# A hybrid decoder step on one core: the keys of heads 6 and 7 computed as a pair of column blocks, their queries projected later, four logit pages moved

## The chip, the cores and the metric

The kernel runs on one core of one Trainium2 chip; the other cores are idle. The metric is device time in microseconds (us): the median over runs of the whole program, lower is better. A core has five engines that run their own instruction streams in order and wait for one another by semaphores: TensorE (PE, matrix products, with PEld for its weight loads), VectorE (DVE), ScalarE (ACT), GpSimd (POOL) and SyncE (SP, which only issues transfers). Accumulators of TensorE are banks of a memory called PSUM.

## The reference

One layer of a decoder step on 528 prompt rows (512 and 16 learned meta rows) and 32 sample rows (8 sequences of 4). Everything is float32.

```
h = rmsnorm(x, g_pre)
q, k, v, ga, cb, cc, ch, gc, ma, mc = split(h @ w_in)     # 2048 x 12288
a = stick_breaking(q, k, v) * silu(ga)                     # 8 heads of 128, strictly causal
c = cb * causal_conv(cc * ch) * silu(gc)
merged = sigmoid(ma + b) * (a @ w_pa) + sigmoid(mc + b) * (c @ w_pc)
y = x + rmsnorm(merged @ w_out, g_post)
```

`stick_breaking` takes logits `z = q.k / sqrt(128) + b_h` and weighs value `s` for query `t` by `sigmoid(z_ts)` times the product of `1 - sigmoid(z_tj)` over the keys `j` between them, in log space. The prompt attends to itself. Each sample sequence attends to 512 cached keys and values (four pages of 128, found by a page table) and to its own four rows. The new keys and values are outputs too.

## The kernel before

**Products.** A float32 matrix is split into two parts of a faster format, `hi` and `lo`, and a product is made of three matrix products: `hi*hi`, `hi*lo`, `lo*hi`. A block of weights is 128 rows of 8 tiles (a `raw` tile, 512 KB). `w_split` (lines 250 to 255) makes `whi` on ScalarE (line 253) and `wlo` on VectorE (line 254); three buffers of each exist (`whl`, line 85: `bufs=3`), so the fourth block has to wait until TensorE has used the first.

**Solo and pair.** A column block of 128 columns of `w_in` costs 2 blocks of weights by 8 tiles by 3 products by 2 halves of the rows: 96 matrix instructions (`gemm`, line 269 of the profile). Two neighbouring column blocks can be done together by `seven` (line 1096, through `pair`, line 1137): a scheme of Strassen's kind, with 7 block products instead of 8, each of 24 instructions (line 1091 of the profile), 168 for two column blocks. It needs sums of weights, made by VectorE into `s` and `raw` (lines 1111 to 1129), sums of the activations (`t_hi`, `t_lo`, made once by `t_sums` and `t_parts`), and differences of results (`c`, lines 1127 and 1132). A pair uses two accumulators `mm` and one `o`; there are three `mm` banks in turn and one `o` bank:

```
def mm_ps():
    return ps.tile([P, 512], F32, tag="mm", name="mm", bufs=3)
```

**Stages.** In order: norm and the queries of heads 0 to 3; `head_now` for heads 0 to 3 (keys, values, the queries of head 4 + h, then the attention of head h); solo column blocks for the keys and values of heads 4 and 5 and the keys of heads 6 and 7 (`tiles`, line 1050), between which the activation sums are made (`STEPS`, line 1056); the values of heads 6 and 7 as the first pair (`later_pair`, line 797); 4 pairs for `ga`, 16 for the convolution, 16 for the gates `ma` and `mc`; then the attention of heads 4 to 7 among the products with `w_pc`, the products with `w_pa`, and `w_out`.

**The samples' attention** (`decode_steps`, line 827) is spread over these stages by `dec_step`. Its first part takes 64 steps, here called pages: one page of cached keys for four heads, 16 instructions on VectorE (line 849, `junk` and `z_all` from `kpage` and `qb`), each a dot product of 128 by 128. `DEC1` and `PAGES` (lines 48 and 779) put the first 5 units of 4 pages behind heads 0 to 3; `dec_group` (line 977), called after each pair, issues the others. When all pages are done, VectorE adds the bias to all logits (lines 879 and 882), ScalarE runs the softplus functions on them (lines 519 to 522) under a function table of its own, and TensorE makes the running sums (lines 895 to 902). Since ScalarE would otherwise change tables again and again, `behind_gates` (line 958) puts the softplus behind the latest sigmoids of the gates, and line 1247 puts each later sigmoid behind the softplus; a sigmoid is also what reads an `mm` or `o` bank of a `ma`/`mc` pair and frees it.

The order of the instructions on each engine is made when the program is built: a scheduler takes what is ready by its own estimates, in the order of the program text where two are ready. On the chip each engine keeps that order.

Of the kernel before, what the change touches and what calls it, by code (L numbers as in the profile page):

```python
# [17 lines left out]
P = 128  # L18
# [24 lines left out]
H = 8  # L43
# [1 line left out]
NPG = 4  # L45
NPOOL = 40
EPS = 1e-6
DEC1 = 5
SCRATCH = 4096
FIRST = 4  # L50
WARM = 8
# [10 lines left out]
def hybrid_step_kernel(  # L62
# [584 lines left out]
    def k_store(h, kr):  # L647
        pool.dma_start(k_scr[h], kr)
# [127 lines left out]
                              start=False, stop=(g == GROUPS[-1] and i == 2), skip_group_check=True)  # L776
        yield ot

    PAGES = ((1, 1, 2, 2), (1, 1, 2, 1), (1, 1, 2, 1), (1, 1, 1, 1))

    def head_now(h):

        qr = hp.tile([P, TQ], F32, name="qr", bufs=2)[:, 0:PQ]
        nc.sync.dma_start(qr, qt_scr[h][:, 0:PQ])
        khi, klo = k_split(np_, k_proj(h))
        dec_step(PAGES[h][0], "part")
        vhi, vlo = v_split(np_, v_proj(h))
        dec_step(PAGES[h][1], "part")
        q_proj(NOW + h)
        dec_step(PAGES[h][2], "part")  # L790
        ot = next(attend(np_, h, khi, klo, vhi, vlo, *q_split(np_, qr)))
        dec_step(PAGES[h][3], "part")
        at = hp.tile([P, TQ], F32, name="qr", bufs=2)[:, 0:PQ]
        act.copy(at, ot)
        pool.dma_start(a_scr[h], at)

    def later_pair(c, h, ready):

        raws = [hp2.tile([P, T], F32, name="raw", bufs=2) for _ in range(2)]
        seen = []  # L800
        for m, half, b in pair(c + h * P, HC, ready):
            act.copy(raws[m][:, NMETA + half * HQ:NMETA + (half + 1) * HQ], b[:, HM:])
            act.copy(raws[m][:, half * HM:(half + 1) * HM], b[:, :HM])
            seen.append(m)
            if seen.count(m) == 2:
                v_store(h + m, v_out(hp2, h + m, raws[m]))

    def head_loads(h, pl):
# [168 lines left out]
    def dec_group():  # L977

        n = n_group[0] = n_group[0] + 1
        if n <= 27:  # L980
            dec_step((0, 2, 2, 2)[n - 1] if n <= 4 else 1 if n <= 20 else 4, "logits")
        else:
            dec_step(2 if n <= 30 else 1)

# [33 lines left out]
    with tc.tile_pool(name="tsum", bufs=2, side="right") as tsp:  # L1018
        r1 = tsp.tile([P, 8, HC], F32, name="r1", bufs=1)

        first_sum = sp2.tile([P, 8, P], F32, name="s")
        held = {}

        def part(x, c, *ij):
            return (blk(x, *ij) if ij else x)[:, c:c + 2]

        def whole(out, c, *ij):
            pin(dve.tensor_add(out, part(h_f, c, *ij), part(l_f, c, *ij)))

        def t_sums(c):  # L1030

            x, y = held[c] = [tsp.tile([P, 2, HC], F32, name=n) for n in "xy"]
            r = part(r1, c)
            whole(y, c, 0, 0)
            whole(r, c, 0, 1)
            pin(dve.tensor_sub(r, y, r))
            whole(x, c, 1, 1)
            pin(dve.tensor_add(x, r, x))
            pin(dve.tensor_sub(y, y, x))

        def t_parts(c):

            x, y = held.pop(c)
            z = tsp.tile([P, 2, HC], F32, name="z", bufs=1)
            whole(z, c, 1, 0)
            pin(dve.tensor_sub(z, z, x))
            for i, src in enumerate((x, y, z)):
                t_split(part(t_hi[i], c), part(t_lo[i], c), src)

        tiles = [(c, h) for h in range(NOW, SOLO) for c in (GATE_K, GATE_V)] + [(GATE_K, h) for h in range(SOLO, H)]  # L1050

        def unit(i, u, pin=lambda ins: ins):
            return w_split(w_load(win_srcs(tiles[i][0] + tiles[i][1] * P)[u]), pin)

        units = {(0, u): unit(0, u) for u in range(2)}
        STEPS = ((), (), ((t_sums, 0), (t_sums, 2)), ((t_parts, 0), (t_sums, 4), (t_parts, 2)),
                 ((t_sums, 6), (t_parts, 4)), ((t_parts, 6),))
        for i, (c, h) in enumerate(tiles):
            if i:
                units[i, 1] = unit(i, 1, pin)  # L1060
            o = gemm([units[i, u] for u in range(2)], h_rhs, ALL)
            if i + 1 < len(tiles):
                units[i + 1, 0] = unit(i + 1, 0, pin)
            for step, n in STEPS[i]:
                step(n)
            if i + 1 == len(tiles):
                first_ws = blocks_of(win, GATE_V + SOLO * P)
                pin(dve.tensor_add(first_sum, first_ws[1], first_ws[2]))
                for n in range(0, 8, 2):
                    t_split(blk(h_hi, 0, 1)[:, n:n + 2], blk(h_lo, 0, 1)[:, n:n + 2], r1[:, n:n + 2])  # L1070
            raw = raw_of(o)
            if c == GATE_K:
                k_store(h, raw)
                k_out(hp, h, raw, qs_all[:, h, :], act.copy)
            else:
                v_store(h, v_out(hp, h, raw, act.copy))
# [71 lines left out]
        yield from seven(ws, n, rb, rt, s, lambda name: sp2.tile([P, HC], F32, name=name)[:, :n], summed=ready is not None)  # L1148

    with tc.tile_pool(name="heads2", bufs=1) as hp2:  # L1150
        later_pair(GATE_V, SOLO, (first_ws, first_sum))
    gp = gctx.enter_context(tc.tile_pool(name="gates", bufs=2))
    up_ = uctx.enter_context(tc.tile_pool(name="convu", bufs=2))

# [484 lines left out]
```

## Time and profile before

| | |
|---|---|
| median of 3 runs | 1569.3 us (1568.15 to 1569.57) |
| the profiled execution | 1568.86 us, its span on the core 1567.3 us |
| granted TensorE clock, mean | 0.998 |
| busy: PE, DVE, ACT, POOL | 1553.9, 1260.7, 760.0, 250.7 us |
| matrix instructions | 12144 |

The profiled execution's time lies 1.6 us above its span (what is ahead of the first and behind the last instruction), and 0.4 us below the median. Busy time adds the stretches in which at least one instruction of an engine is under way; since matrix instructions overlap in the pipeline, their own durations (0.29 us) are longer than the step from one start to the next (0.13 us), and prices are taken from steps. The stages by time: norm and queries to about 73 us, heads 0 to 3 and solo blocks to 338, the first pair to 360, `ga` and the convolution to about 788, the gates to about 1150, and the rest to the end.

### The profile page before, as it was taken

What the parts mean: (1) busy time and instruction counts of PE and PEld (TensorE: products, weight loads), DVE (VectorE), ACT (ScalarE), POOL (GpSimd) and SP (SyncE); (2) the same over time, 40 slices, a digit from 0 to 9 for tenths busy, and PEclk for the clock granted to TensorE, in tenths of its full rate; (3) what the DMA queues carried; (4) which work ended last, traced back from release to release, by engine and by line L of the source; (5) the groups of instructions that cost most, each with busy time, mean ns of one, the idle gap of its engine ahead of it and who ended that gap; (6) DMA issues with size and microseconds to landing.
All of it is one profiled execution on the core that took longest, in us unless ns stands there. A gap on an engine that the chain in (4) does not pass through costs nothing.

```text
span 1567.3 us, 32349 instructions
## 1 busy us (share of the span) xinstructions
PE 1553.9 (99%) x12144; PEld 1519.2 (97%) x12144; DVE 1260.7 (80%) x3572; ACT 760.0 (48%) x1367; POOL 250.7 (16%) x426
## 2 busy tenths in 40 slices
PE   9999999999999999999999999999999999999997
PEld 8999999999999999999999999989899999999997
DVE  7239997776799999999999999665668868877686
ACT  7245555544444444444444446544466643355563
POOL 4223332222111010001111111332200010000000
PEclk9999999999999999999999999999999999999999
DMA  9255554345554445445455654666694555433345
GB/s 272 81 170 161 162 168 124 95 127 152 165 174 147 140 129 161 133 137 170 121 170 169 186 158 142 226 222 218 199 325 159 173 160 168 153 114 90 102 142 188
DMA packets 300650, 252.77 MB, mean 161 GB/s; under 512 B 11509, under 2 KB 268585, under 8 KB 299677
## 3 DMA queue, kind: packets, MB, share of 16 engines
q1 hardware_dynamic: 272021, 160.45, 34.8%
q0 software_dynamic: 28368, 89.98, 17.3%
q8 instruction: 95, 1.56, 0.4%
q14 instruction: 62, 0.51, 0.1%
q10 hardware_dynamic: 104, 0.27, 0.1%
HBM read 217.95 MB, written 32.71 MB: 160 GB/s over the span
## 4 chain that ended last, share of the span: by engine, by line
PE 95%; DVE 2%; DMA 1%; ACT 0%; issue 0%; SPq 0%; POOL 0%; DVEq 0%; ACTq 0%
PE mm L1091 34%; PE mm L269 27%; PE o L1091 25%; PE z L763 1%; PE o L775 1%; PE z L334 1%; PE tp L924 1%; DMA xt<-in_x_prompt 1%; PE z L681 1%; PE mm L346 1%; DMA raw<-in_w_in 1%; PE tp L558 0%; PE z L1424 0%; PE mm L334 0%; DVE wlo L254 0%
## 5 line engine op out<-in xcount | busy, mean ns | idle before, releaser
L253 ACT CAST whi<-raw 128x1024 fp32r<-128x1024 f32 x247 | 259.2, 1051 | 305.8 <-PE mm L1091 90.7
L254 DVE TENSOR_TENSOR wlo<-raw,whi 128x1024 fp32r<-128x1024 f32 x247 | 301.6, 1223 | 102.9 <-ACT whi L253 100.9
L1091 PE MATMUL mm<-h_hi,whi 128*128 128x272 f32 (+2 forms) x1184 | 342.6, 290 | 0.3 <-ACT whi L253 0.3
L1091 PE MATMUL mm<-h_lo,whi 128*128 128x272 f32 (+2 forms) x1184 | 341.8, 289 | 0.0
L1091 PE MATMUL mm<-h_hi,wlo 128*128 128x272 f32 (+2 forms) x1184 | 341.1, 290 | 0.1
L1091 PE MATMUL o<-t_hi,wlo 128*128 128x272 f32 (+2 forms) x888 | 257.1, 290 | 0.0
L1091 PE MATMUL o<-t_hi,whi 128*128 128x272 f32 (+2 forms) x888 | 257.0, 289 | 0.0
L1091 PE MATMUL o<-t_lo,whi 128*128 128x272 f32 (+2 forms) x888 | 256.1, 288 | 0.0
L849 DVE CUSTOM_DVE_ANT_0 junk<-kpage,qb 128x128 f32<-128x128 f32 x1024 | 244.7, 286 | 3.5 <-DMA qb<-q_scr 3.0
L1091 PEld LDWEIGHTS mm<-h_hi,whi 128*128 128x128 f32 x1184 | 223.6, 189 | 5.6 <-issue 2.5
L1091 PEld LDWEIGHTS mm<-h_lo,whi 128*128 128x128 f32 x1184 | 222.8, 188 | 0.9 <-issue 0.8
L1091 PEld LDWEIGHTS mm<-h_hi,wlo 128*128 128x128 f32 x1184 | 222.6, 189 | 1.0 <-DVE wlo L254 0.9
L253 ACT CAST whi<-s 128x1024 fp32r<-128x1024 f32 x129 | 135.4, 1050 | 154.0 <-PE o L1091 53.0
L254 DVE TENSOR_TENSOR wlo<-s,whi 128x1024 fp32r<-128x1024 f32 x129 | 157.4, 1220 | 61.9 <-ACT whi L253 61.7
L269 PE MATMUL mm<-h_lo,whi 128*128 128x280 f32 (+1 forms) x576 | 168.7, 293 | 0.0
L269 PE MATMUL mm<-h_hi,wlo 128*128 128x280 f32 (+1 forms) x576 | 168.6, 293 | 0.0
L269 PE MATMUL mm<-h_hi,whi 128*128 128x280 f32 (+1 forms) x576 | 168.3, 292 | 0.0
L1091 PEld LDWEIGHTS o<-t_hi,wlo 128*128 128x128 f32 x888 | 166.9, 188 | 0.9 <-DVE wlo L254 0.9
L1091 PEld LDWEIGHTS o<-t_hi,whi 128*128 128x128 f32 x888 | 167.3, 188 | 0.2
L1091 PEld LDWEIGHTS o<-t_lo,whi 128*128 128x128 f32 x888 | 167.3, 188 | 0.0
L269 PEld LDWEIGHTS mm<-h_lo,whi 128*128 128x128 f32 x576 | 108.3, 188 | 0.7
L269 PEld LDWEIGHTS mm<-h_hi,whi 128*128 128x128 f32 x576 | 108.4, 188 | 0.6
(473 smaller groups left out, 3124.1 us busy)
## 6 DMA issues: line engine op xcount, KB each, us to landing
raw<-in_w_in SPq DMA_DIRECT2D x192, 512.0 KB, 4.7
kpage<-in_cache_k POOLq DMA_DIRECT2D x64, 256.0 KB, 3.5
qb<-q_scr POOLq DMA_DIRECT2D x32, 512.0 KB, 5.6
vpage<-in_cache_v POOLq DMA_DIRECT2D x64, 256.0 KB, 5.4
raw<-in_w_out SPq DMA_DIRECT2D x32, 512.0 KB, 3.8
gate_scr<-g POOLq DMA_DIRECT2D x32, 272.0 KB, 3.1
gt<-gate_scr POOLq DMA_DIRECT2D x16, 544.0 KB, 4.2
raw<-in_w_pc SPq DMA_DIRECT2D x16, 512.0 KB, 4.6
```

The costliest lines, as they stand in the source:

```text
L253: act.copy(hi, x)
L254: low[0] = pin(dve.tensor_sub(lo, x, hi.bitcast(F32)))
L269: pe.matmul(o, lhsT=w, rhs=r[:, t0:t1], start=(k == 0 and n == 0), stop=(k == nk - 1 and n == 2))
L334: pin(pe.matmul(o, lhsT=l, rhs=r[:, k, t0:t1], start=(start and m == 0), stop=(stop and m == 2), skip_group_check=True))
L346: pin(pe.matmul(q_o[h], lhsT=l, rhs=(h_lo if m == 1 else h_hi)[:, k, START[0][0]:START[0][1]], start=(k == 0 and m == 0 and h % 2 == 0), s ...
L681: pe.matmul(zt[:m, c0:c0 + n], lhsT=l[:, s0:s0 + m], rhs=r[:, ts:ts + n], start=(c0 == 0 and i == 0), stop=(i == 2), skip_group_check=True)
L763: pe.matmul(o, lhsT=l, rhs=x, start=False, stop=(i == len(ops) - 1), skip_group_check=True)
L775: pe.matmul(ot[:, ts - NMETA:ts - NMETA + n], lhsT=l[:m, st, :], rhs=x[:m, c0:c0 + n], start=False, stop=(g == GROUPS[-1] and i == 2), ski ...
L849: dve.tensor_tensor_reduce(out=junk, in0=kt[:, h * P:(h + 1) * P], in1=qt[:, t, h * P:(h + 1) * P], scale=1.0, scalar=0.0, op0=ALU.mult, o ...
L924: pin(pe.matmul(po[32 * j:32 * (j + 1), :], lhsT=lhs, rhs=rhs, start=(pg == 0), stop=last and n >= len(vts) - 4, tile_position=(0, 32 * j) ...
L1091: pe.matmul(o, lhsT=l[:, k, :], rhs=r, start=(start and k == 0 and m == 0), stop=(stop and k == 7 and m == 2), skip_group_check=True)
```

## The change

The keys of heads 6 and 7 leave the list of solo blocks and become the first pair; the values of heads 6 and 7 follow as the second. `later_pair` therefore handles keys as well (it stores them and makes the key outputs), and takes the sample queries of heads 6 and 7 from a small tile `qs`, loaded back from memory, because the tile that held all of them is gone by then. The queries of heads 6 and 7 are no longer projected in `head_now(2)` and `head_now(3)` but in the block behind `head_now(3)`; the activation sums start two solo blocks earlier in the list (`STEPS` loses its two empty entries). Four of the 20 pages behind the heads move to the pairs: `DEC1` goes from 5 to 4, `PAGES` is cut to 16, and `dec_group` issues 3, 4 and 3 pages instead of 2, 2 and 2 after its second, third and fourth pair.

```
-DEC1 = 5
+DEC1 = 4
...
-    PAGES = ((1, 1, 2, 2), (1, 1, 2, 1), (1, 1, 2, 1), (1, 1, 1, 1))
+    PAGES = ((1, 1, 1, 2), (1, 1, 2, 1), (1, 1, 0, 1), (0, 0, 0, 3))
...
-        q_proj(NOW + h)
+        if NOW + h < SOLO:
+            q_proj(NOW + h)
...
-        at = hp.tile([P, TQ], F32, name="qr", bufs=2)[:, 0:PQ]
+        at = hp.tile([P, T if h == NOW - 1 else TQ], F32, name="raw" if h == NOW - 1 else "qr", bufs=2)[:, 0:PQ]
...
-    def later_pair(c, h, ready):
+    def later_pair(c, h, qs=None, ready=None):
...
-            if seen.count(m) == 2:
+            if seen.count(m) < 2:
+                continue
+            if qs is not None:
+                k_store(h + m, raws[m])
+                k_out(hp2, h + m, raws[m], qs[:, m, :])
+            else:
                 v_store(h + m, v_out(hp2, h + m, raws[m]))
...
-            dec_step((0, 2, 2, 2)[n - 1] if n <= 4 else 1 if n <= 20 else 4, "logits")
+            dec_step((0, 3, 4, 3)[n - 1] if n <= 4 else 1 if n <= 20 else 4, "logits")
...
-        tiles = [(c, h) for h in range(NOW, SOLO) for c in (GATE_K, GATE_V)] + [(GATE_K, h) for h in range(SOLO, H)]
+        tiles = [(c, h) for h in range(NOW, SOLO) for c in (GATE_K, GATE_V)]
...
+        for h in range(SOLO, H):
+            q_proj(h)
         units = {(0, u): unit(0, u) for u in range(2)}
-        STEPS = ((), (), ((t_sums, 0), (t_sums, 2)), ((t_parts, 0), (t_sums, 4), (t_parts, 2)),
+        STEPS = (((t_sums, 0), (t_sums, 2)), ((t_parts, 0), (t_sums, 4), (t_parts, 2)),
                  ((t_sums, 6), (t_parts, 4)), ((t_parts, 6),))
...
-            if i:
+            if i > 1:
                 units[i, 1] = unit(i, 1, pin)
...
+            if i == 0:
+                units[1, 1] = unit(1, 1, pin)
...
-                first_ws = blocks_of(win, GATE_V + SOLO * P)
+                first_ws = blocks_of(win, GATE_K + SOLO * P)
...
-        later_pair(GATE_V, SOLO, (first_ws, first_sum))
+        qs = hp2.tile([P, H - SOLO, TS], F32, name="qs")
+        for h in range(SOLO, H):
+            pool.dma_start(qs[:, h - SOLO, :], qt_scr[h][:, PQ:TQ])
+        later_pair(GATE_K, SOLO, qs, (first_ws, first_sum))
+        later_pair(GATE_V, SOLO)
```

Line numbers of the changed program are 10 to 14 higher from line 803 on. What the built programs hold, engine by engine, at three places follows; numbers behind a name tell one buffer's use from another's.

TensorE, where the keys of heads 6 and 7 are made. Before, a solo block (line 269) goes over both halves of the rows with one weight block after the other:

```order
L269 MATMUL mm_4643<-h_hi_89,whi_4583 128x280
L269 MATMUL mm_4643<-h_lo_90,whi_4583 128x280
...
L269 MATMUL mm_4795<-h_hi_89,wlo_4792 128x280
L269 MATMUL mm_4796<-h_hi_89,whi_4743 128x280
L269 MATMUL mm_4796<-h_lo_90,whi_4743 128x280
```

Now the pair (line 1101, which was 1091) stands there:

```order
L1101 MATMUL mm_4508<-h_hi_89,whi_4511 128x280
L1101 MATMUL mm_4508<-h_lo_90,whi_4511 128x280
L1101 MATMUL mm_4508<-h_hi_89,wlo_4512 128x280
...
L1101 MATMUL o_4510<-t_hi0_3615,wlo_4570 128x280
L1101 MATMUL o_4510<-t_hi0_3615,whi_4569 128x280
```

The two key blocks took 192 instructions of 128x280, the pair takes 168; of no other matrix shape does the count change.

VectorE, where the last pages end, in a `ma`/`mc` pair (called A below; it is the pair whose accumulators are `mm_13493`, `mm_13494` before and `mm_13497`, `mm_13498` now, and the next pair is B). Before:

```order
L254 TENSOR_TENSOR wlo_13526<-s_13492,whi_13525 128x1024
...
L1114 TENSOR_TENSOR s_13492<-s_13492,raw_13484 128x1024
...
L849 ISA junk_12955,z_all_908<-kpage_12923,qb_12590 128x128
L849 ISA z_all_908 128x1
L879 COPY dS_13426<-bsb_868 128x256
L882 TENSOR_TENSOR z_all_908<-z_all_908,dS_13426 128x256 x4
L254 TENSOR_TENSOR wlo_13556<-s_13492,whi_13555 128x1024
L254 TENSOR_TENSOR wlo_13586<-raw_13490,whi_13585 128x1024
```

Now (lines 849, 879, 882 are 855, 885, 888), with 25 pairs of the `L855` rows where two stand at the ends of the marked stretch:

```order
L254 TENSOR_TENSOR wlo_13847<-raw_13751,whi_13846 128x1024
L1139 TENSOR_TENSOR s_13753<-s_13753,raw_13751 128x1024
L855 ISA junk_12909,z_all_908<-kpage_12893,qb_12592 128x128
...
L855 ISA junk_12959,z_all_908<-kpage_12927,qb_12594 128x128
L885 COPY dS_13430<-bsb_868 128x256
L888 TENSOR_TENSOR z_all_908<-z_all_908,dS_13430 128x256 x4
...
L1142 TENSOR_TENSOR c_13681<-mm_13498,s2_13617 128x272
...
L254 TENSOR_TENSOR wlo_13879<-raw_13747,whi_13878 128x1024
```

The last page's instructions stood ahead of pair A's third weight block; they now stand behind pair B's fourth, 25 of them in one run. From the end of the pairs for heads 6 and 7 up to here, VectorE's rows are the same in both programs, but for a `junk` row that changes places with a neighbour in three of the pairs; so the four pages that left the heads' stage come out at the far end, as 64 more such instructions between pair A's third block and pair B's fourth.

TensorE and ScalarE at the same place. Before, TensorE's running sums (`z`) stand ahead of pair A's last product:

```order
L1091 MATMUL mm_13494<-h_hi_89,wlo_13650 128x272
L895 MATMUL z_13452<-dS_13426,neg_u_88 32x256
L901 MATMUL z_13455<-dr_13424,neg_u_88 128x256
L902 MATMUL z_13455<-dS_13426,neg_one_86 128x256
L901 MATMUL z_13460<-dr_13424,neg_u_88 128x256
L1091 MATMUL o_13495<-t_hi2_4041,whi_13680 128x272
```

Now they stand behind pair B's first product (accumulator `mm_13754`, with `whi_13757`) and ahead of its second (`mm_13755`):

```order
L1101 MATMUL mm_13754<-h_hi_89,wlo_13758 128x272
L901 MATMUL z_13456<-dS_13430,neg_u_88 32x256
L907 MATMUL z_13459<-dr_13428,neg_u_88 128x256
L908 MATMUL z_13459<-dS_13430,neg_one_86 128x256
L907 MATMUL z_13464<-dr_13428,neg_u_88 128x256
L1101 MATMUL mm_13755<-h_hi_89,whi_13786 128x272
```

ScalarE now has, one behind the other and with no weight block between them, the fourth block of B, the softplus of the new rows (`z_new`), that of all pages in two halves, the table load and the sigmoids of pair A:

```order
L253 CAST whi_13846<-raw_13751 128x1024
L519 ACTIVATE de_13426<-z_new_909,zero_c_80 32x256
...
L519 ACTIVATE de_13426<-z_all_908,zero_c_80 128x512
L520 ACTIVATE de_13426<-de_13426 128x512
L521 ACTIVATE dl_13427<-de_13426,one_c_82 128x512
L522 ACTIVATE dr_13428<-z_all_908,zero_c_80 128x512
...
L1262 ACT_TABLE_LOAD
L1262 ACTIVATE g_13486<-mm_13497,bg_869 128x272
L1262 ACTIVATE g_13487<-c_13649,bg_869 128x272
```

Before, three weight blocks (`whi_13617`, `whi_13649`, `whi_13680`) stood among the rows of the softplus. What moved at this place: the whole step from logits to running sums, by a little less than one pair, and with it what stands ahead of it and behind it on the three engines.

## The prediction

> **What bounds the kernel now.** I read the page first, then the list of what TensorE waits for, then the busy time by stage.
>
> ```profile
> span 1567.3 us, 32349 instructions
> PE 1553.9 (99%) x12144; PEld 1519.2 (97%) x12144; DVE 1260.7 (80%) x3572; ACT 760.0 (48%) x1367; POOL 250.7 (16%) x426
> PE 95%; DVE 2%; DMA 1%; ACT 0%; issue 0%; SPq 0%; POOL 0%; DVEq 0%; ACTq 0%
> ```
>
> The third line is the chain of waits: 95% of it is TensorE. The list of TensorE's waits has five entries; the first and the last are:
>
> ```profile
> PE mm L151 <- DVE neg_one L115: 1.4, 1, 1.4
> ...
> PE mm L1091 <- ACT whi L253: 0.3, 1, 0.3
> ```
>
> The first stands at the start, and 0.3 us is all that TensorE waits in the pairs. So TensorE's own instructions set the time, each one removed is time gained, and each wait that the change adds is time lost, since no slack lies behind it to take it up. The busy time by stage (each column: us busy and instructions, in the order PE, PEld, DVE, ACT, POOL, then clock, DMA share, GB/s):
>
> ```profile
> 142.00:245.00 103.00, 103.00 (x783) 99.86 (x783) 99.07 (x565) 54.92 (x108) 33.91 (x66) 1.00 0.58 174
> 245.00:338.00 93.00, 93.00 (x718) 91.09 (x716) 69.30 (x131) 47.72 (x100) 22.09 (x41) 1.00 0.35 103
> 338.00:360.00 22.00, 22.00 (x173) 21.74 (x172) 13.41 (x14) 10.83 (x22) 4.01 (x7) 1.00 0.56 158
> 360.00:424.00 64.00, 64.00 (x512) 63.86 (x511) 44.93 (x96) 30.95 (x46) 12.08 (x20) 1.00 0.54 164
> 424.00:958.00 534.00, 533.68 (x4220) 531.71 (x4219) 517.06 (x1793) 235.85 (x351) 58.26 (x101) 1.00 0.51 152
> ```
>
> VectorE is full in two of them: 99 of 103 us behind the heads, and 517 of 534 from the second `ga` pairs to the end of the pages. It keeps up, but it has no room there.
>
> **Term 1, the pair.** 192 matrix instructions of 280 columns become 168. A row of the chain from the solo blocks gives the step:
>
> ```profile
> 319.31 9.13 PE mm L269 x71
> ```
>
> 9.13 / 71 = 0.129 us, so 24 of them are 3.1 us less. The pair's extra work on VectorE (three more `wlo` at 1.13 us, three more sums, two differences) has room: a pair of this width left 22.00 - 13.41 = 8.6 us free above. This term has no other price.
>
> **Term 2, the heads' stage, costed at nothing.** The queries of heads 6 and 7 are not removed, only issued later, and two key blocks (2 x 96 x 0.129 = 24.7 us of TensorE) leave. From 142 to 338 us TensorE had 196 us, VectorE 99.07 + 69.30 = 168.4. Now TensorE has 171.3; VectorE loses 64 dot products at 0.21 us and four `wlo` at 1.13 us (both steps below), 18.0 in all, and needs 150.4: 88% where it was 86%. The cover of this stage is thus as good as before; if it were gone, the most that could show is one query block per head, 2 x 96 x 0.129 = 24.7 us, the least is nothing. I take nothing, because the share hardly moves. The transfers of `qs` stand on POOL behind the solo blocks' outputs and land a whole pair before TensorE asks for them.
>
> **Term 3, four more pages behind pairs.** 64 dot products at 0.21 us are 13.4 us of VectorE. In 360:424 it had 64.00 - 44.93 = 19 us free, so the time is there, but the order of its instructions does not use it: the rows of these pairs are the same as before, and the 64 come out at the end. What happens there is seen in VectorE's rows around the last pages of the kernel before:
>
> ```profile
> 960.09 0.28 DVE L849 CUSTOM_DVE_ANT_0 junk<-kpage,qb 128x128 f32<-128x128 f32 x1
> 960.30 0.29 DVE L849 CUSTOM_DVE_ANT_0 junk<-kpage,qb 128x128 f32<-128x128 f32 x1
> 960.63 0.29 DVE L879 COPY dS<-bsb 128x256 f32<-128x256 f32 x1
> 960.96 1.44 DVE L882 TENSOR_TENSOR z_all<-z_all,dS 128x256 f32<-128x256 f32 x4
> 962.31 1.22 DVE L254 TENSOR_TENSOR wlo<-s,whi 128x1024 fp32r<-128x1024 f32 x1
> 963.44 1.22 DVE L254 TENSOR_TENSOR wlo<-raw,whi 128x1024 fp32r<-128x1024 f32 x1
> ```
>
> Steps from start to start: a dot product 0.21, the copy 0.33, the four bias sums 1.35, a block (`wlo` or a sum of weights) 1.13. ScalarE in the same stretch, first the softplus of the new rows, then that of the pages, the table, a sigmoid of pair A:
>
> ```profile
> 963.92 1.05 ACT L253 CAST whi<-raw 128x1024 fp32r<-128x1024 f32 x1 [0.95 <-PE mm L1091]
> ...
> 965.46 0.51 ACT L521 ACTIVATE dl<-de,one_c 32x256 f32<-32x256 f32 x1
> 965.87 0.49 ACT L522 ACTIVATE dS<-z_new,zero_c 32x256 f32<-32x256 f32 x1
> 966.27 0.71 ACT L519 ACTIVATE de<-z_all,zero_c 128x512 f32<-128x512 f32 x1
> 967.01 0.63 ACT L520 ACTIVATE de<-de 128x512 f32<-128x512 f32 x1
> 967.55 1.03 ACT L253 CAST whi<-s 128x1024 fp32r<-128x1024 f32 x1
> ...
> 968.76 0.72 ACT L521 ACTIVATE dl<-de,one_c 128x512 f32<-128x512 f32 x1
> 969.39 0.71 ACT L522 ACTIVATE dr<-z_all,zero_c 128x512 f32<-128x512 f32 x1
> 970.00 0.71 ACT L519 ACTIVATE de<-z_all,zero_c 128x512 f32<-128x512 f32 x1
> 970.62 1.03 ACT L253 CAST whi<-raw 128x1024 fp32r<-128x1024 f32 x1
> 971.55 0.63 ACT L520 ACTIVATE de<-de 128x512 f32<-128x512 f32 x1
> ...
> 973.57 1.28 ACT L1248 ACT_TABLE_LOAD   x1
> 974.87 0.49 ACT L1248 ACTIVATE g<-mm,bg 128x272 f32<-128x272 f32 x1
> ```
>
> And TensorE:
>
> ```profile
> 976.01 0.61 PE L895 MATMUL z<-dS,neg_u 32*32 32x256 f32 x2
> ...
> 977.77 0.48 PE L1091 MATMUL o<-t_hi,whi 128*128 128x272 f32 x1
> ...
> 980.97 0.28 PE L1091 MATMUL mm<-h_hi,whi 128*128 128x272 f32 x1
> 981.22 0.29 PE L1091 MATMUL mm<-h_hi,whi 128*128 128x272 f32 x1
> ```
>
> Before, the running sums (1.76 us, 976.01 to 977.77) found their inputs ready, and the bank that pair A's first result held was free at 974.87 + 0.49 = 975.4; pair B asks for it with its second accumulator at 981.22. The margin was 5.9 us, and the pages now end 13.4 us of VectorE time later. The new order ties this to TensorE itself. The last 25 dot products stand behind `wlo_13847`, pair B's fourth block. It is made from `whi_13846`, which takes the buffer of B's first block and so waits until TensorE is through B's first product: the wait of 0.95 us on `PE mm` at 963.92 is one of this kind. And on TensorE the running sums, and behind them B's second accumulator, stand right behind that first product. So TensorE must stand still while the rest of the chain runs. From the end of B's first product, t0:
>
> - `whi_13846` 1.05, `wlo_13847` 1.13, a sum of weights 1.13, 25 dot products 5.25: 8.6
> - copy and bias sums, 0.33 + 1.35: 10.2; meanwhile four steps of 0.41 (965.46 to 965.87) on the new rows, which wait for the last page only
> - eight functions on the pages; the pieces between the weight blocks are 1.28 (966.27 to 967.55), 1.86 (968.76 to 970.62) and 2.02 (971.55 to 973.57): 5.2, so 15.4
> - table load to sigmoid 1.30 and the sigmoid 0.49: 17.2
>
> B's second accumulator starts at t0 + 17.2, where it would start at t0 + 1.76 behind the running sums alone: 15.4 us lost. Behind TensorE, `wlo` of B's later blocks, which wait for it, are late by as much, and the stages after are bound by TensorE too, so nothing gives it back. t0 itself is 980.97 - 1.76 (the sums no longer stand ahead of it) - 3.1 + 24 x 0.125 (the step at 980.97: 0.25 for two) = 979.1.
>
> The bounds: if the running sums alone hold TensorE and not the bank, they cannot start before the first half's functions are done, 10.2 + 2.6 = 12.8 after t0, and 12.8 is the loss. If ScalarE takes as long from the last page to the sigmoid as it did before with blocks in between (960.30 + 0.21 to 974.87, 14.4), it is 8.6 + 14.4 + 0.49 - 1.76 = 21.7. I take 15.4, since no block stands in between now.
>
> **Term 4, the clock after the stand.** Up to there TensorE runs without a pause. What a pause does is seen at the two ends of the run:
>
> ```profile
> 1.36 3.78 PE L151 MATMUL mm<-neg_one 128*128 128x512 f32 x8 [1.36 <-DVE neg_one L115]
> ...
> 6.22 0.46 PE L163 MATMUL o<-g_hl,pick 128*128 128x512 f32 x1
> ...
> 7.45 2.70 PE L151 MATMUL mm<-neg_one 128*128 128x512 f32 x11
> 9.99 0.27 PE L229 MATMUL mm<-ident,hn 128*128 128x128 f32 x1
> ```
>
> ```profile
> 1558.00:1560.00 2.00, 0.00 (x0) 0.00 (x0) 0.91 (x3) 1.38 (x5) 0.00 (x0) 0.86 0.95 322
> 1560.00:1567.30 7.30, 0.00 (x0) 0.00 (x0) 2.19 (x3) 0.00 (x0) 0.00 (x0) 0.50 0.70 253
> ```
>
> The granted clock falls to 0.50 within some 2 us of TensorE's last work, and at the start the first 11 instructions of 512 columns take (6.22 - 1.36) / 11 = 0.44 us each where later ones take (9.99 - 7.45) / 11 = 0.23. So a stand of 15 us ends at half clock, and the first 4.9 us of work behind it lose about half: 2.4 us. Bounds: nothing, if the few running sums wake it, and 4.9, if it takes twice as long.
>
> The Trainium skill ("TensorE: Matmul & The Clock Gate", Part 1) says that one idle window of about 3.4 us halves the clock and about 3.4 us of sustained work restores it. By that this term would be about 1.7 us, an estimate from that page, and the total 1583.3 us. The trace agrees on the half clock (0.44 against 0.23 us); its slow stretch of 4.9 us is longer, and I keep that.
>
> **The sum.** Profiled execution 1568.86 - 3.1 + 15.4 + 2.4 = 1583.6; the median of runs lies 0.4 higher: 1584.0 us, 0.9% slower. With both lower bounds 1579.0 (1569.3 - 3.1 + 12.8), with both upper ones 1592.8 (1569.3 - 3.1 + 21.7 + 4.9).
>
> **Rivals.** (1) *The pages fit, and only term 1 remains*: 1566.2 us, on the other side. It needs the softplus of pair A to be done within the 5.9 us margin, so the pages to end no later than about 7 us behind their old place. For it: 19 us of free VectorE time in 360:424, more than the 13.4 needed. Against it: the order puts 25 of the 64 behind a wait for TensorE, and an engine does not reorder. (2) *The stand is there but short*, if the bank is not in the way and the half clock costs nothing: 1579.0 as above, or less if VectorE's dot products in an idle machine step faster than 0.21. (3) *The heads' stage loses its cover too*: the attention of heads 2 and 3 leans on the query blocks that moved; up to 24.7 us more, so up to 1609. Against it: the shares, 88% and 86%. (4) *The pair does not save what it says*: sums of weights late in the two first pairs would cost what a `wlo` costs, 1.13 us apiece; 1585 to 1587, inside the range.
>
> **Chances.** The forecast with its bounds, 1579 to 1592: 0.75. Rival 1: 0.12, half of it faster by over 0.2%, half within. Rival 2 below 1579, slower: 0.08. Rival 3: 0.05. The measurement tells about 0.2% (3.1 us) from no change; so faster 0.06, same 0.06, slower 0.88. The range that leaves out no more than 0.2: 1576 to 1591.
>
> **What would show it.** In the profile after: a run of 25 dot products on VectorE near 982 to 988, with no block between them; TensorE idle for about 14 to 17 us from about 979, put down to VectorE's `dr` or ScalarE's sigmoid; a granted clock below 1 right behind it; 12120 matrix instructions; the first pair at about 313 us, and pair B's first product at about 976 instead of 980.97. I am wrong if TensorE's list of waits has nothing of over 5 us near there, and then most likely because the scheduler's order is met by a bank or a buffer that is free sooner than I read.

## The result, and the profile after

The changed kernel takes 1585.95 us (median of 4 runs, 1585.26 to 1586.64), the kernel before 1568.88 us on the same chip: a ratio of 1.0109, 95% interval 1.0091 to 1.0126. It is 17.1 us slower; the forecast was 1584.0 us. The profiled execution took 1585.98 us, 17.1 more than that of the kernel before.

The page of the changed kernel, first the span, the busy time and the chain of waits:

```profile
span 1584.4 us, 32331 instructions
PE 1552.9 (98%) x12120; PEld 1517.2 (96%) x12120; DVE 1269.8 (80%) x3585; ACT 762.8 (48%) x1369; POOL 256.3 (16%) x428
PE 95%; DVE 2%; DMA 1%; issue 1%; ACT 0%; POOL 0%; DVEq 0%; SPq 0%; ACTq 0%; POOLq 0%
```

TensorE has 24 instructions less, and the span is 17.1 us longer than its 1567.3 us before. Where the 17.1 us went is read in one view, the list of what TensorE waits for (us in total, times, longest):

```profile
PE z L901 <- POOL dS L876: 15.5, 1, 15.5
PE mm L151 <- DVE neg_one L115: 1.4, 1, 1.4
PE z L627 <- ACT raw L617: 1.3, 1, 1.3
```

The first line is new, and so is the third; the second stands at the start, as before. (What a line names is the instruction that came last by the profile: the mask on POOL; what set its time is followed below.) The long wait in VectorE's rows:

```profile
981.66 1.22 DVE L254 TENSOR_TENSOR wlo<-raw,whi 128x1024 fp32r<-128x1024 f32 x1
982.80 1.22 DVE L1139 TENSOR_TENSOR s<-s,raw 128x1024 f32<-128x1024 f32 x1
983.94 0.28 DVE L855 CUSTOM_DVE_ANT_0 junk<-kpage,qb 128x128 f32<-128x128 f32 x1
...
989.20 0.28 DVE L855 CUSTOM_DVE_ANT_0 junk<-kpage,qb 128x128 f32<-128x128 f32 x1
...
989.53 0.29 DVE L885 COPY dS<-bsb 128x256 f32<-128x256 f32 x1
989.86 1.43 DVE L888 TENSOR_TENSOR z_all<-z_all,dS 128x256 f32<-128x256 f32 x4
```

and in ScalarE's (in brackets the idle time ahead of a row and what ended it):

```profile
979.82 1.04 ACT L253 CAST whi<-raw 128x1024 fp32r<-128x1024 f32 x1
989.53 0.51 ACT L519 ACTIVATE de<-z_new,zero_c 32x256 f32<-32x256 f32 x1 [8.66 <-DVE z_all L855]
...
991.78 0.51 ACT L522 ACTIVATE dS<-z_new,zero_c 32x256 f32<-32x256 f32 x1 [0.77 <-DVE dS L890]
992.20 0.70 ACT L519 ACTIVATE de<-z_all,zero_c 128x512 f32<-128x512 f32 x1
...
997.59 1.28 ACT L1262 ACT_TABLE_LOAD   x1
998.89 0.49 ACT L1262 ACTIVATE g<-mm,bg 128x272 f32<-128x272 f32 x1
```

and in TensorE's, with its clock in three stretches (us busy and instructions of PE, PEld, DVE, ACT, POOL, then clock, DMA share, GB/s):

```profile
979.58 0.29 PE L1101 MATMUL mm<-h_hi,wlo 128*128 128x272 f32 x1
995.32 1.06 PE L901 MATMUL z<-dS,neg_u 32*32 32x256 f32 x2 [15.45 <-POOL dS L876]
997.03 1.22 PE L907 MATMUL z<-dr,neg_u 128*128 128x256 f32 x2 [0.65 <-DVE dr L528]
...
999.43 0.75 PE L1101 MATMUL mm<-h_hi,whi 128*128 128x272 f32 x1
```

```profile
979.80:995.30 15.50, 0.07 (x1) 0.00 (x0) 14.57 (x73) 5.95 (x11) 1.94 (x2) 0.65 0.42 121
995.30:1001.40 6.10, 5.43 (x16) 3.95 (x17) 5.29 (x11) 5.96 (x11) 0.67 (x2) 0.50 0.01 3
1001.40:1010.00 8.60, 8.60 (x65) 8.39 (x65) 3.20 (x6) 3.98 (x6) 2.28 (x3) 1.00 0.38 124
```

TensorE is through B's first product at 979.58 + 0.125 = 979.7 and starts its second accumulator at 999.43. Between them lie the 25 dot products, the softplus, the table load and A's sigmoid, which ends at 998.89 + 0.49 = 999.38. VectorE is busy 14.57 of the 15.5 us in which TensorE stands.

### The profile page after: what moved, and what is told of

It reads as the page before. It is cut to its first block, busy times and chain, and to the rows that moved or that the text cites. A ratio compares the mean times of both kernels' runs of the same rounds, so it can differ in the third digit from the quotient of the medians.

```text
span 1584.4 us, 32331 instructions
## 1 busy us (share of the span) xinstructions
PE 1552.9 (98%) x12120; PEld 1517.2 (96%) x12120; DVE 1269.8 (80%) x3585; ACT 762.8 (48%) x1369; POOL 256.3 (16%) x428
## 4 chain that ended last, share of the span: by engine, by line
PE 95%; DVE 2%; DMA 1%; issue 1%; ACT 0%; POOL 0%; DVEq 0%; SPq 0%; ACTq 0%; POOLq 0%
PE mm L1101 35%; PE o L1101 26%; PE mm L269 25%; DMA raw<-in_w_in 1%; PE o L775 1%; PE z L763 1%; PE z L334 1%; PE tp L930 1%; PE z L681 1%; PE mm L346 1%; PE tp L558 0%; PE z L1438 0%; PE mm L334 0%; DVE junk L855 0%; DVE x_n L1480 0%
## 5 line engine op out<-in xcount | busy, mean ns | idle before, releaser
L1101 PE MATMUL mm<-h_hi,whi 128*128 128x272 f32 (+2 forms) x1216 | 352.6, 290 | 0.0
L1101 PE MATMUL mm<-h_hi,wlo 128*128 128x272 f32 (+2 forms) x1216 | 351.4, 291 | 0.1
L1101 PE MATMUL mm<-h_lo,whi 128*128 128x272 f32 (+2 forms) x1216 | 351.2, 289 | 0.0
L855 DVE CUSTOM_DVE_ANT_0 junk<-kpage,qb 128x128 f32<-128x128 f32 x1024 | 243.8, 284 | 3.7 <-DMA qb<-q_scr 3.5
L1101 PEld LDWEIGHTS mm<-h_hi,whi 128*128 128x128 f32 x1216 | 230.0, 189 | 4.4 <-issue 2.5
L1101 PEld LDWEIGHTS mm<-h_lo,whi 128*128 128x128 f32 x1216 | 229.3, 189 | 0.9 <-issue 0.8
L269 PE MATMUL mm<-h_lo,whi 128*128 128x280 f32 (+1 forms) x512 | 149.9, 293 | 0.0
L269 PE MATMUL mm<-h_hi,whi 128*128 128x280 f32 (+1 forms) x512 | 149.5, 292 | 0.0
L269 PE MATMUL mm<-h_hi,wlo 128*128 128x280 f32 (+1 forms) x512 | 149.2, 293 | 0.0
L269 PE MATMUL mm<-c_hl,whi 128*128 128x272 f32 x512 | 100.8, 289 | 0.0
L831 POOL DMA_DIRECT2D kpage<-in_cache_k x64 | 35.5, 555 | 397.9 <-DVE z_all L855 385.1
```

Of the source, the lines that this page charges most:

```text
L269: pe.matmul(o, lhsT=w, rhs=r[:, t0:t1], start=(k == 0 and n == 0), stop=(k == nk - 1 and n == 2))
L831: return pool.dma_start(t, cache[bass.ds(page_reg[i], 1), :, cs].rearrange("o s c -> (o s) c"))
L855: dve.tensor_tensor_reduce(out=junk, in0=kt[:, h * P:(h + 1) * P], in1=qt[:, t, h * P:(h + 1) * P], scale=1.0, scalar=0.0, op0=ALU.mult, o ...
L1101: pe.matmul(o, lhsT=l[:, k, :], rhs=r, start=(start and k == 0 and m == 0), stop=(stop and k == 7 and m == 2), skip_group_check=True)
```

## The experiments

**The pages alone, the pair alone, the queries alone.** First the kernel before with nothing but the four pages moved (lines of the change that touch `DEC1`, `PAGES` and the counts of `dec_group`).

> The kernel before with the four pages moved and nothing else (DEC1, PAGES and the counts behind the ga pairs as in the change; no pair for the keys, queries where they were). In the built order the last 25 dot products stand behind pair B's fourth block and the running sums behind B's first product, as in the change. My theory: the stand of 15.5 us and what follows it come whole without the pair, so the time is that of the change plus what the pair saves: 1586.0 + 3.1 = 1589 us (1587 to 1590). Rival b (the stand needs the pair): 1569 us. Rival c (the lost time is made up of the stand and of a loss that the pair brings elsewhere): clearly under 1587 us.

1586.98 us, ratio 1.0111 (1.0094 to 1.0128). Its list of waits:

```profile
PE z L895 <- POOL dS L870: 15.3, 1, 15.3
```

The stand comes whole, without the pair: rivals b and c fall. That it lies only 1.0 us above the change, where 3.1 were expected, is inside the intervals of the two; the wait of 1.25 us on `raw` is in the change's list and not in this one, and the half clock behind the stand ends earlier here, after three slow steps of B's second accumulator (1000.65 to 1001.62 us).

Then the change with the pages as they were before, that is, the pair together with the moved queries (against the changed kernel):

```
-DEC1 = 4
+DEC1 = 5
-    PAGES = ((1, 1, 1, 2), (1, 1, 2, 1), (1, 1, 0, 1), (0, 0, 0, 3))
+    PAGES = ((1, 1, 2, 2), (1, 1, 2, 1), (1, 1, 2, 1), (1, 1, 1, 1))
-            dec_step((0, 3, 4, 3)[n - 1] if n <= 4 else 1 if n <= 20 else 4, "logits")
+            dec_step((0, 2, 2, 2)[n - 1] if n <= 4 else 1 if n <= 20 else 4, "logits")
```

> The change with the pages left as before (20 behind the heads, 2, 2 and 2 behind the ga pairs); the pair and the moved queries stay. The last page then stands where it stood before, ahead of pair A's third weight block, and the running sums ahead of A's last product. My theory (the four pages cost the time, the pair saves 24 x 0.129 us): no wait of TensorE over 2 us after the start, 1569 - 3 = 1566 us. Rival a (the heads' stage, with two query blocks less to lean on and all 20 pages, loses its cover): waits of TensorE between 142 and 338 us, and up to 1590 us. Rival b (the stand comes from the pair itself, which moves the gates by 3 us against the pages): a wait of some 15 us near 980, 1584 us.

1571.72 us, ratio 1.0018 (1.0009 to 1.0028): slower than before, and 5.7 us above my 1566. No stand near 980, so rival b falls here too, but rival a holds:

```profile
PE z L681 <- ACT qhi L547: 1.3, 1, 1.3
PE z L627 <- ACT raw L617: 1.3, 1, 1.3
PE z L681 <- DVE qlo L548: 0.9, 1, 0.9
```

Between 245 and 338 us TensorE is busy 89.53 of 93 us. Whether this is the pair or the queries, the kernel before tells with the queries alone moved:

```
-        q_proj(NOW + h)
+        if NOW + h < SOLO:
+            q_proj(NOW + h)
...
+        for h in range(SOLO, H):
+            q_proj(h)
         units = {(0, u): unit(0, u) for u in range(2)}
```

(with the output of head 3's attention in a `raw` tile, as in the change).

> The kernel before with the queries of heads 6 and 7 projected behind head 3 and nothing else (20 pages stay behind the heads, all keys solo). The prediction's term 2 (moving the queries costs nothing): 1569 us and no new wait. What the pair alone with all its pages showed (waits of TensorE for qhi, qlo and raw of 3.5 us together in the heads' stage and a lower clock behind two of them) says that these come from the queries' leaving the heads' stage and not from the pair: waits of 2 to 4 us between 230 and 290 us, the last dot products where they were, and 1572 to 1575 us.

1573.36 us against 1569.23, ratio 1.0033 (1.0020 to 1.0046), and the same three lines with the same numbers stand in its list. So the queries' leaving costs 4.1 us as long as all 20 pages stay in the heads' stage; with four pages gone, the change keeps only the 1.3 us of `raw`. The last of this row is the pair with nothing else. Against the change with 20 pages, above:

```
-        if NOW + h < SOLO:
-            q_proj(NOW + h)
+        q_proj(NOW + h)
...
-        for h in range(SOLO, H):
-            q_proj(h)
         units = {(0, u): unit(0, u) for u in range(2)}
```

(and the output of head 3's attention in a `qr` tile again).

> The keys of heads 6 and 7 as a pair and nothing else: the queries of heads 6 and 7 stay behind heads 2 and 3, all 20 pages stay where they were. The prediction's term 1 alone (24 products less at 0.129 us, no other price): 1568.9 - 3.1 = 1565.8 us, no wait over 1 us behind the start, since the queries cover the attention of heads 2 and 3 as before and the last page ends where it did. Rival i (the pair saves less than its products, because the activation sums now have four solo blocks instead of six to be made behind): weight blocks or activation sums late between 260 and 340 us, 1567 to 1570 us.

1579.28 us, ratio 1.0068 (1.0054 to 1.0081). That is 10.7 us above the kernel before (1568.56). Its wait, a row of ScalarE, and VectorE's rows at that place:

```profile
PE mm L269 <- DVE wlo L254: 11.1, 1, 11.1
```

```profile
291.48 0.59 ACT L794 COPY qr<-o 128x512 f32<-128x512 f32 x1 [4.54 <-PE o L775]
```

```profile
292.66 0.74 DVE L1019 TENSOR_TENSOR t_lo<-x,t_hi 128x560 fp32r<-128x560 f32 x1 [5.15 <-ACT t_hi L1018]
...
294.62 0.73 DVE L1033 TENSOR_TENSOR y<-h_hi,h_lo 128x560 f32<-128x560 f32 x1
...
301.64 0.73 DVE L1019 TENSOR_TENSOR t_lo<-z,t_hi 128x560 fp32r<-128x560 f32 x1
302.29 2.35 DVE L254 TENSOR_TENSOR wlo<-raw,whi 128x1024 fp32r<-128x1024 f32 x2
```

The activation sums (`t_sums`, `t_parts`) now have only four solo blocks to be made behind. VectorE works on them from 292.66 to 302.29 us while the `wlo` that TensorE needs stands behind them. It starts late, too: it sits idle for 5.15 us until ScalarE makes `t_hi`, which stands behind ScalarE's copy of head 3's attention, and that waits for TensorE. In the changed kernel the two query blocks lie ahead of the solo blocks and no such wait is in its list. Rival i is right in its mechanism and far too small in its price.

**When do the pages end?** Two versions of the change move only the end of the logits. The first does the 16 dot products of the very last page twice, which makes the run of 25 one of 41:

```
-                        for i, qt in enumerate(qts):
+                        for i, qt in enumerate(qts * (2 if (hf, b, pg) == (1, DB - 1, NPG - 1) else 1)):
+                            i = i % 2
```

> The change with the 16 dot products of the very last page done twice (same values, written again). In the built order the run of 25 dot products behind pair B's fourth block becomes 41; nothing else moves. My theory (the stand ends when the chain behind the last dot product ends): the wait of TensorE grows by 16 x 0.21 = 3.4 us to 18.9 us, the time from 1586.0 to 1589.4 us. Rival d (the stand is due to the place of the running sums behind pair B's first product, or to the bank, not to when the pages end): the wait stays 15.5 us and the time 1586 us.

1588.91 us, ratio 1.0126 (1.0110 to 1.0141), and the wait:

```profile
PE z L902 <- POOL dS L877: 18.9, 1, 18.9
```

3.4 us more stand for 3.4 us of VectorE, and some 3 us more time. The second issues four pages earlier, behind the first `ga` pairs:

```
-            dec_step((0, 3, 4, 3)[n - 1] if n <= 4 else 1 if n <= 20 else 4, "logits")
+            dec_step((2, 4, 4, 4)[n - 1] if n <= 4 else 1 if n <= 20 else 4, "logits")
```

> The change with 2, 4, 4 and 4 pages behind the ga pairs where it has 0, 3, 4 and 3. In the built order 32 dot products leave the end of the pages; the last two now stand ahead of the bias sums, behind the sum L1124 that ran at 977.48 us in the change; the running sums stand where they stand in the change, behind B's first product. My theory (TensorE waits for the end of the logits, step by step): bias copy at 977.48 + 1.13 + 0.42 = 979.0 instead of 989.5 us, everything behind it 10.4 us earlier, less up to two weight blocks of 1.13 us that VectorE now has between; the wait of TensorE shrinks from 15.5 to 5 to 8 us, the time to 1586.0 - 10.4 = 1575.6, up to 1578 us. Rival d (what holds the running sums is their place in the order, not the lateness of the pages): 1586 us. Rival e (VectorE is full from 424 us on, the 32 come out late all the same): 1584 us or more.

1579.87 us (lowest 1577.62), ratio 1.0062 (1.0045 to 1.0079). The rows of TensorE:

```profile
982.50 0.29 PE L1101 MATMUL mm<-h_hi,wlo 128*128 128x272 f32 x1
991.62 1.05 PE L901 MATMUL z<-dS,neg_u 32*32 32x256 f32 x2 [8.83 <-POOL dS L876]
...
994.97 0.79 PE L1101 MATMUL mm<-h_hi,whi 128*128 128x272 f32 x1
```

From the end of B's first product (982.6) to its second accumulator it is 12.3 us where the change has 19.7: 7.4 less, near what the theory with its two blocks has (10.4 - 2 x 1.13 = 8.1). Rivals d and e fall. Pair A's sigmoid ends at 994.02 here, 0.95 us ahead of the second accumulator: in this run the running sums at half clock hold TensorE, and not the bank. The time gained is less than that, since in the profiled execution TensorE is already 2.9 us later at the end of B's first product; where half of these come from is told in the last section.

**Room for the four pages.** VectorE had idle time ahead of 424 us, and the counts behind the `ga` pairs do not reach all of it. Two pages issued between the two pairs do:

```
         later_pair(GATE_K, SOLO, qs, (first_ws, first_sum))
+        dec_step(2, "logits")
         later_pair(GATE_V, SOLO)
```

> The change with two more pages issued between the key pair and the value pair of heads 6 and 7 (the counts behind the ga pairs stay 0, 3, 4 and 3). In the built order the last dot product stands ahead of pair A's first weight block and the running sums inside A's second accumulator. My theory: the logits are done before TensorE asks for the sums, no wait over 2 us, and only the pair's 3 us are left: 1566 us. Rival e (VectorE has no room for the four pages anywhere in the pairs): weight blocks come late between 338 and 980 us and the time is 1570 to 1580 us. Rival a (the heads' stage loses cover): as in the change, there is nothing of it in its list of waits, so nothing here.

1567.50 us, ratio 0.9990 (0.9980 to 1.0000). All that TensorE waits for longer than 0.6 us behind the start:

```profile
PE z L627 <- ACT raw L617: 1.3, 1, 1.3
```

The stand is gone and with it 18.4 us of the change (1585.95 - 1567.50). VectorE took the pages up between 338 and 424 us, here first in this version and then in the change:

```profile
338.00:424.00 86.00, 86.00 (x686) 85.81 (x685) 75.83 (x269) 40.54 (x65) 20.04 (x34) 1.00 0.60 182
```

```profile
338.00:424.00 86.00, 86.00 (x684) 85.82 (x685) 60.30 (x119) 40.59 (x64) 15.74 (x26) 1.00 0.51 155
```

15.5 us more of VectorE's work, none of it waited for. Rival e falls.

**What is left, the wait on `raw`.** Three more versions try to take that 1.25 us away from the last one. The first copies the attention of head 3 out of its bank behind the first solo block's copies instead of ahead of them (`head_now` returns the tile and the bank of head 3):

```
             raw = raw_of(o)
+            if i == 0:
+                act.copy(*last_at)
+                pool.dma_start(a_scr[NOW - 1], last_at[0])
```

> The version with two pages between the two pairs, and the copy of head 3's attention out of its bank issued behind the copies of the first solo key block instead of ahead of them; the key outputs' product L627 then stands inside the next block. My theory (the 1.25 us wait of TensorE on raw, L617, and the half clock that follows it in some executions, are what is left of the change's cost): no wait over 1 us behind the start, 1567.5 - 1.3 - up to 1 = 1565.2 to 1566.2 us. Rival h (the wait moves elsewhere, since the attention's bank is freed later): 1567.5 us with a new entry in the list of waits.

1569.55 us, ratio 1.0003 (0.9994 to 1.0012). The wait is gone, and this one has come:

```profile
PE mm L269 <- DVE wlo L254: 2.9, 1, 2.9
```

The second makes the values of heads 4 and 5 ahead of their keys, and runs beside a repetition of the version with two pages between:

```
-        tiles = [(c, h) for h in range(NOW, SOLO) for c in (GATE_K, GATE_V)]
+        tiles = [(c, h) for h in range(NOW, SOLO) for c in (GATE_V, GATE_K)]
```

> The version with two pages between the two pairs, and the values of heads 4 and 5 made ahead of their keys in the list of solo blocks. In the built order the first product that needs the copies of a solo block's banks then stands 15 instructions (15 x 0.129 = 1.9 us) behind the attention of head 3, where the product L627 stood right behind it. My theory (that wait of 1.25 us, and the half clock behind it in some executions, is what is left of the price of the moved queries): no wait of 1 us behind the start, 1567.5 - 1.3 = 1566.2 us, which is what the prediction's rival 1 gave for the pair's saving alone. Rival h (the wait turns up elsewhere, as when the copy was put behind): 1567.5 us or more with a new entry.

> The version with two pages between the two pairs once more, on the chip of the run with the values first, to compare the two: 1567.5 us as before, one wait of 1.25 us on raw.

1567.96 us, ratio 0.9994 (0.9985 to 1.0003), against 1567.54 us, ratio 0.9991 (0.9982 to 1.0000). The product no longer waits, but the next block's does, for the bank that the same copies have to empty:

```profile
PE mm L269 <- ACT raw L617: 1.3, 1, 1.3
```

Rival h both times: what is late is the copy on ScalarE, not what asks for it first. Its rows in the change show why; the copy of head 3's attention, which waits for TensorE, stands ahead of the copies of the block:

```profile
278.06 0.59 ACT L795 COPY raw<-o 128x512 f32<-128x512 f32 x1 [1.96 <-PE o L775]
278.54 0.82 ACT L617 COPY raw<-mm 128x272 f32<-128x272 f32 x4
```

The third keeps the queries behind heads 2 and 3, with the same lines undone as in the pair with nothing else.

> The version with two pages between the two pairs, with the queries of heads 6 and 7 kept behind heads 2 and 3 (16 pages behind the heads). If the wait of 1.25 us on raw comes from the moved queries, it is gone here: 1567.5 - 1.3 = 1566.2 us or, with the half clock behind it gone in all executions, 1565.7 us. Rival h (the wait comes from the pair's order of the solo blocks): 1567.5 us and the wait still there.

1578.08 us, ratio 1.0061 (1.0048 to 1.0075): no wait on `raw`, but 9.7 us on `wlo`, as in the pair with nothing else.

**The clock term.** Six matrix instructions whose result is not used go ahead of the running sums:

```
+                    pw = z_ps()[:, :BHT]
+                    for _ in range(6):
+                        pe.matmul(pw, lhsT=neg_u.bitcast(F32), rhs=flat(z_all[:, 0]), start=True, stop=True)
                     pn = z_ps()[:TS, :BHT]
```

> The change with six matrix instructions of 128x256 (result not used) ahead of the running sums, which can start once the bias sums are done, about 991.3 us, so that TensorE works for the last 4 us of its stand. By half-clock steps of 0.88 us they end near 996.5, before the running sums of the pages can start at 997.03. My theory: the running sums and pair B's second accumulator then run at full clock; the sums end at about 998.4 instead of 999.43 us, but the second accumulator still waits for pair A's sigmoid at 999.38, so only the slow steps behind 999.43 are saved: 1.1 us, 1584.9 us. Rival f (the bank does not hold it, the sums alone do): 2.1 us saved, 1583.9 us, and no wait on the sigmoid. Rival g (the clock costs nothing, or work in half the stand does not wake it): 1586.0 us and steps of 0.225 us as before.

1585.89 us, ratio 1.0105 (1.0089 to 1.0120); the time does not tell 1.1 us from nothing. The rows do:

```profile
990.85 4.33 PE L902 MATMUL z<-z_all,neg_u 128*128 128x256 f32 x12 [10.47 <-DVE z_all L888]
...
998.50 0.59 PE L910 MATMUL z<-dr,neg_u 128*128 128x256 f32 x2
999.94 0.39 PE L1104 MATMUL mm<-h_hi,whi 128*128 128x272 f32 x1 [0.84 <-ACT g L1265]
1000.17 0.29 PE L1104 MATMUL mm<-h_lo,whi 128*128 128x272 f32 x1
1000.29 0.29 PE L1104 MATMUL mm<-h_hi,wlo 128*128 128x272 f32 x1
```

The steps are 0.125 us, so rival g falls as to the clock. The sums are done some 0.8 us earlier than the bank, and TensorE then waits for the sigmoid: the bank holds it, and rival f falls. In the change the sums at half clock (995.32 to 999.43) end within 0.05 us of the sigmoid, so their slowness costs nothing and only the slow steps behind 999.43 count.

## Why the prediction was right

**Term 1, the pair, 3.1 us.** The count is 12120 as said, the first pair starts at 312.77 us (predicted about 313) and B's first product at 976.68 (about 976). t0 was predicted at 979.1 and is 979.7, so pair and moved queries together saved 2.5 us up to there, not 3.1 (the 1.25 us of term 2 are already in the 2.5; what gave a part of them back is not traced). The version with two pages between saves 1.3 to 1.4 us over the whole kernel, which agrees with 3.1 less the wait of 1.25 us and what the clock adds to it in some executions (last section). "This term has no other price" was wrong: alone, the pair has one of 11 us (the activation sums), which the moved queries pay.

**Term 2, nothing.** In the change it is 1.25 us (`raw`), so nearly right, for a reason that the runs contradict. The step "the cover of this stage is thus as good as before", read from 88% against 86%, is the weak one: with the queries alone moved VectorE is busy 98.71 + 64.98 of the same 196 us, 84%, and TensorE waits 3.5 us. The rows show what counts instead of the share, the order on ScalarE: for `raw`, its copy of head 3's attention stands ahead (above); for `qhi` of head 3, with the queries alone moved, its copy of head 2's attention (245.31 us) stands ahead of the cast that TensorE waits for (245.79). The forecast came out because the four pages had left as well.

**Term 3, 15.4 us.** Right in its mechanism but for the first link: each run that moved the end of the logits moved the stand (pages alone, one page twice, pages earlier, pages between). The size was 19.7 - 1.76 = 18.0 us. By steps from t0: the bias copy starts at 989.53, 9.8 behind t0 where 8.6 was predicted. `whi_13846` came when predicted, but VectorE was still at earlier rows, so `wlo_13847` started at 981.66 and not at 980.9: VectorE itself, not the buffer that TensorE frees, set that point. Then the pages' functions start at 992.20, not 1.7 but 2.7 us behind the bias copy: the fourth step on the new rows waits 0.77 us for the cleared `dS`, and the pages' functions stand behind it on ScalarE. The functions (5.4) and table and sigmoid (1.8) are as predicted. 1.2 + 1.0 + 0.2 is 2.4 of the 2.6 us by which the term was too small. The list names POOL's mask as what ended the wait, a step the chain left out; it does not set the end, since the running sums of the pages need `dr`, which comes at 997.03, and the bank comes at 999.38.

**Term 4, 2.4 us.** The clock was 0.50 from 995.3 to 1001.4. But most of that lay under the wait for the bank; what shows is from 999.43 on, 2.2 us for the first nine steps (999.43 to 1001.61) where nine of 0.125 take 1.1, so 1.1 us. The term was twice too large and made up for half of what term 3 lacked.

Sum by what was measured: -2.5 + 18.0 + 1.1 = 16.6 of 17.1 us. Forecast: 14.7, with a first term, a third and a fourth that missed by 0.6, 2.6 and 1.3 us and in part made up for one another, so that the total is closer than its terms. TensorE's last row starts at 1551.08 us before and at 1567.71 now, 16.6 us later, and lasts 5.96 us in both: the sum is whole on TensorE, and the other 0.5 us lies behind it, where the last outputs are finished and written.

**The rivals.** Rival 1 (the pages fit) is what the program would have done with two pages between the pairs: its condition, room for 13.4 us in VectorE ahead of 424 us, was there, and the order did not use it. Rival 3's mechanism exists, as the queries alone show; the change escapes most of it by the pages that it moves. Rival 2 falls with the stand of 19.7 us and a half clock that shows; of rival 4 there is nothing in the change's list, which has no wait in the two first pairs.

## What to carry to other kernels

A change of several parts may be a balance: here the pair needs the queries as cover for its sums, and the queries need the pages gone, so none of the three is priced by itself, and the part that paid for the others was put where it cost 18 us. Before work is handed to an engine's free time, look in the built order whether its rows land there; free time ahead of a full stretch is worth nothing to rows that come out behind it. Two pages issued one pair earlier give a kernel of 1567.5 us, 1.3 to 1.4 us below the one before, in two measurements with an interval that ends at 1.0000, so that this gain is at the edge of what the runs tell.

## What the runs showed of the hardware

A wait of 1.25 us can be followed by half clock, and in another execution is not. The same product behind the same wait, first in the change and then in the version with the pages earlier:

```profile
279.27 0.25 PE L627 MATMUL z<-qs_all,raw 128*32 128x32 f32 x2 [1.25 <-ACT raw L617]
...
279.68 0.30 PE L269 MATMUL mm<-h_lo,whi 128*128 128x280 f32 x1
279.82 0.29 PE L269 MATMUL mm<-h_hi,wlo 128*128 128x280 f32 x1
```

```profile
279.85 0.25 PE L627 MATMUL z<-qs_all,raw 128*32 128x32 f32 x2 [1.25 <-ACT raw L617]
...
280.41 0.44 PE L269 MATMUL mm<-h_lo,whi 128*128 128x280 f32 x1
280.65 0.44 PE L269 MATMUL mm<-h_hi,wlo 128*128 128x280 f32 x1
```

In the second the steps are 0.233 us for 3.4 us (to 283.45), which costs some 1.5 us: half of the 2.9 us by which that execution is late. It also happened in the profiled executions of the change with 20 pages and of the repeated version with two pages between; not in the first of that version, nor with the queries alone, one page twice and in the run on the clock. The Trainium skill ("TensorE: Matmul & The Clock Gate", on the oscillation of the gate) puts the limit at idle gaps of over some 3.4 us; here a wait of 1.25 us was followed by half clock in three of the eight profiled executions that have it. The Trainium skill also says (same page, Part 1) that the gate looks at a window that runs freely; that would fit a wait that is punished only in some executions, but no run here shows the window. The two waits on `qhi` and `qlo` (1.29 and 0.93 us, up to 246.73 and 248.47 in the change with 20 pages) were not followed by it, there or with the queries alone. In the change with 20 pages the clock stays at 1.00 from 245 to 280 us: it falls behind one of the three waits, and not behind two, as the expectation for the queries alone says.

Behind the long stands the half clock lasted 5.0 to 6.3 us, where the start has 4.9: 6.1 us behind 15.5 us (995.3 to 1001.4, in which TensorE still waited for 0.65), 5.0 us behind 15.3 us (the pages alone, 996.54 to 1001.55), 6.3 us behind 18.9 us (one page twice) and, behind 11.1 us, 6.0 us of work without a pause (the pair with nothing else, 303.56 to 309.55). The length of the stand alone does not tell it, since 15.3 and 15.5 us are followed by 5.0 and 6.1.
